# A hybrid encoder step on one core: the convolved tile gets a second buffer, the first tile's products are reordered, and the next tokens' norm is issued earlier

## The chip, the cores and the metric

One core of a Trainium2 chip runs the whole kernel. The metric is device time in microseconds (us), the median of several executions. The engines are TensorE (PE, the matmuls, with its weight loads PEld), VectorE (DVE), ScalarE (ACT), GpSimd (POOL) and SyncE (SP), which issues the DMA transfers. Each engine runs its own queue of instructions in order and waits on semaphores for the others.

## The reference

One layer of a streaming encoder is applied to 2048 prompt tokens and to 32 further tokens of a running stream. The width is 1024. Phase one, which the change is about, is the mixer's input side:

```python
proj = rmsnorm(x, g_mix_pre) @ w_in            # q, k, v: 512 each; z: 512; xbc: 768; dt: 8
xbc_c, conv_new = causal_dwconv(xbc, conv_prev, w, b)   # width 4, along the tokens
xbc_c = silu(xbc_c)                            # 512 of x, 128 of B, 128 of C
dt = softplus(dt_raw + dt_bias)
y, h_fin = ssd_scan(x, dt, -exp(a_log), B, C, h0)       # a state carried from chunk to chunk
y = rmsnorm((y + d_skip * x) * silu(z), g_ssm_out)
```

Then come stick-breaking attention of 8 heads over q, k and v, the output projection, and a GeLU-gated MLP with a convolution of width 3. All arithmetic is float32.

## The kernel before, in words

**Products.** A float32 matrix product is made of three in a faster 32-bit format (`F32R`): each operand is divided into a high part and a low remainder, and high by high, high by low and low by high are summed in PSUM. For the tokens these parts are `xhi[k]` and `xlo[k]`, for k = 0 to 7 (8 x 128 = 1024 rows), in one buffer each (`parts`). For the weights `divide` makes them: ACT writes the high part (L145), POOL the low one (L146). `dense` (L152) issues 24 products of one output tile: for each k, the three in a row.

**Blocks of tokens.** `phase_in` runs over four blocks (`SBS`): three of 512 tokens and a last one of 544. For each block s it does, in the order of the source:

1. `split`: ACT writes xhi from the normalised tokens `x` (L319), DVE the low parts xlo (L320). Block 0 has a helper of its own, `first` (L334, L335).
2. Six output tiles of xbc, in the order c = 4, 5, 0, 1, 2, 3. Each is evicted by ACT into `raw` (L377), convolved by DVE into `xc[:, c]` (L384 and three times L388), and multiplied by its sigmoid (ACT L392, DVE L393). `xc` comes from the pool `kn.xcp`, which has one buffer.
3. v and dt (L412): four or five groups of 128 tokens, two halves of 24 products each, evicted by ACT (L419, L421). In block 0 `load_wv` brings their weights just before.
4. The scan's scalars (L443 to L471), with small products into PSUM tiles `st`, and then the scan itself by groups of 128 tokens (L478 to L562). It reads and overwrites `xc`. The row `acD` goes out to memory and comes back spread over all partitions (`acB`, `eA`).
5. `prep(s + 1)`, not in the last block: four DMA loads of the next tokens into `x` (L299), their squares on ACT (L303, L306) summed by POOL (L307), the root through two PSUM tiles `st` (`rstd_steps`: PE L203, DVE L216, POOL L226, PE L238, ACT L248), and eight DVE products that normalise `x` in place (L310).
6. Four tiles of k and four of q: evicted by ACT or DVE (L352, L350), divided by ACT and POOL (L584, L585), and stored.
7. `gate`: four tiles of z, whose sigmoid multiplies `xc` (ACT L627, DVE L628, L630); and `gate_norm`: squares (L641 to L645), a root (L177 to L183), DVE products on `xc` (L650), and its two parts, made by ACT (L654) and POOL (`klo`, L656) and stored. In the last block these two steps are left to the attention stage.

**Order.** All of it is traced in the order of the source, and then a scheduler puts each engine's instructions in a fixed order by a simulated timeline; the source order is the priority. A tile of a pool is waited for until the last reader of the buffer's previous tile is through. The sizes that matter: the product tiles `o` have two PSUM buffers (shared by steps 2, 3, 6 and 7), `st` has two, and `x`, `raw` and `xc` have one buffer each.

Later stages (attention of all heads, with the rest of the layer as filler work between its steps) keep `xc` until the last block's gate is done, and are not touched by the change.

Of the kernel before, what the change touches and what calls it, by code (L numbers as in the profile page):

```python
# [8 lines left out]
F32 = mybir.dt.float32  # L9
# [22 lines left out]
P = 128  # L32
# [37 lines left out]
class Kernel:  # L70
# [81 lines left out]
    def parts(self):  # L152
        return tuple([self.xp.tile([P, 544], F32R, name=f"{e}{k}") for k in range(KC)] for e in ("xhi", "xlo"))

    def dense(self, ps, w, x, c0, c1, k0=0, first=True, last=True, pin=False, loose=False):
        nc = self.nc
        xhi, xlo = x
        for k, (whi, wlo) in enumerate(w):
            hi, lo = xhi[k0 + k][:, c0:c1], xlo[k0 + k][:, c0:c1]
            for i, (l, r) in enumerate(((whi, hi), (whi, lo), (wlo, hi))):  # L160
                mm = nc.tensor.matmul(  # L161
                    ps[:, : c1 - c0], l, r,
                    start=first and i == 0 and k == 0,
                    stop=last and i == 2 and k == len(w) - 1,
                    **({"skip_group_check": True} if loose else {}),
                )
                if pin and i == 0 and k == 0:
                    self.pin(mm)
        if pin:
            self.mark(mm)  # L170

# [81 lines left out]
def phase_in(kn, ctx):  # L253
    nc, tc, a, o = kn.nc, kn.tc, kn.a, kn.o
# [39 lines left out]
    def prep(s):  # L294

        t0, nt = SBS[s]
        x = ep.tile([P, KC, 544], F32, name="x")
        for k in range(0, KC, 2):
            nc.sync.dma_start(x[:, k : k + 2, :nt], a["xT"][:, k : k + 2, t0 : t0 + nt])  # L299
        sq = tmp.tile([P, 544], F32, name="sq", bufs=1)  # L300
        for k in range(KC):
            if k == 0:
                nc.scalar.activation(sq[:, :nt], x[:, k, :nt], AF.Square)  # L303
            else:
                t = tmp.tile([P, 550], F32, name="t")
                nc.scalar.activation(t[:, :nt], x[:, k, :nt], AF.Square)  # L306
                nc.gpsimd.tensor_tensor(sq[:, :nt], sq[:, :nt], t[:, :nt], op=ALU.add)  # L307
        r = kn.rstd_narrow(rp, psm, "st", [sq], nt, D)
        for k in range(KC):
            nc.vector.scalar_tensor_tensor(  # L310
                x[:, k, :nt], x[:, k, :nt], kn.col(C_GMIX + k), r[:, :nt], op0=ALU.mult, op1=ALU.mult
            )
        return x

    def split(s, x):
        nt = SBS[s][1]
# [38 lines left out]
    for s, (t0, nt) in enumerate(SBS):  # L355
        last = s == NSB - 1
        if s == 0:
            xs, r0 = first()
            rcol = kn.rcol
        else:  # L360
            xs = split(s, nxt)
        xhi, xlo = xs
        raw = ep.tile([P, 6, 550], F32, name="raw")
        xc = kn.xcp.tile([P, 6, 547], F32, name="xc")
        W = 547 if last else 512
        nc.vector.tensor_copy(raw[:, :, 0:3], hist[:])
        if last:
# [3 lines left out]
        for c in (4, 5, 0, 1, 2, 3):  # L371
            w = wfirst if s == 0 and c == 4 else kn.weight(wp, a["wbx"][c])
            for c0, c1 in tiles_of(nt):
                ps = psd.tile([P, 512], F32, name="o")
                kn.dense(ps, w, xs, c0, c1)
                e = min(c1, 512)
                nc.scalar.copy(raw[:, c, 3 + c0 : 3 + e], ps[:, : e - c0])  # L377
                if c1 > 512:
                    nc.scalar.copy(raw[:, c, 518:550], ps[:, e - c0 : c1 - c0])
            if s == 0:  # L380
                nc.vector.tensor_tensor(raw[:, c, 3 : 3 + nt], raw[:, c, 3 : 3 + nt], r0[:, :nt], op=ALU.mult)
            y = xc[:, c, :W]
            wc = C_SW + c * 4
            nc.vector.tensor_scalar(  # L384
                y, raw[:, c, 0:W], kn.col(wc), kn.col(C_SB + c), op0=ALU.mult, op1=ALU.add
            )
            for i in range(1, 4):
                nc.vector.scalar_tensor_tensor(  # L388
                    y, raw[:, c, i : i + W], kn.col(wc + i), y, op0=ALU.mult, op1=ALU.add
                )  # L390
            t = tmp.tile([P, 550], F32, name="t")
            nc.scalar.activation(t[:, :W], y, AF.Sigmoid)  # L392
            nc.vector.tensor_tensor(y, y, t[:, :W], op=ALU.mult)  # L393
# [3 lines left out]
        else:  # L397
            nc.vector.tensor_copy(hist[:], raw[:, :, 512:515])

        if s == 0:  # L400
            load_wv()
        nb = 5 if last else 4
# [3 lines left out]
        for b in range(nb):  # L406
            q = min(P, nt - b * P)
            vp = [psd.tile([P, 512], F32, name="o") for _ in range(2)]
            for h in range(2):
                for k in range(KC):  # L410
                    for i, (l, rr) in enumerate(((xhi, wv[0]), (xlo, wv[0]), (xhi, wv[1]))):
                        nc.tensor.matmul(  # L412
                            vp[h][:q, :260], l[k][:, b * P : b * P + q], rr[:, k, h * 260 : h * 260 + 260],
                            start=i == 0 and k == 0, stop=i == 2 and k == KC - 1,
# [40 lines left out]
        ps = psm.tile([P, 512], F32, name="st")  # L455
# [10 lines left out]
        ps = psm.tile([P, 512], F32, name="st")  # L466
# [6 lines left out]
        for b in range(nb):  # L473
# [22 lines left out]
            for g in range(2):  # L496
                rows = slice(g * 64, g * 64 + 64)
                nc.tensor.matmul(cy[:q, g, :q], xc[rows, 4, sl], xc[rows, 5, sl], start=True, stop=True)
                for i in range(2):
# [3 lines left out]
                        start=True, stop=True,  # L503
# [15 lines left out]
            ps = psm.tile([P, 512], F32, name="st")  # L519
# [11 lines left out]
            ps = psm.tile([P, 512], F32, name="st")  # L531
# [16 lines left out]
            ps = psm.tile([P, 512], F32, name="st")  # L548
# [19 lines left out]
            nc.sync.dma_start(o["ssm"][0], hT[state["h"]][:])  # L568
            nc.sync.dma_start(o["ssm"][1], hS[:])

        if not last:
            nxt = prep(s + 1)
        for name, dst in (("wk", kn.kS), ("wq", kn.qS)):
            for c in range(4):
                w = kn.weight(wp, a[name][c])
                hi = so.tile([P, 544], F32, name="khi")[:].bitcast(F32R)
                lo = so.tile([P, 544], F32, name="klo")[:].bitcast(F32R)
                kf = so.tile([P, 544], F32, name="kf")
                for c0, c1 in tiles_of(nt):
                    ps = psd.tile([P, 512], F32, name="o")  # L580
# [1039 lines left out]
```

## Time and profile before

| | us |
|---|---|
| median of 3 runs | 2937.35 |
| lowest and highest | 2936.06, 2943.05 |
| the profiled execution | 2941.02 |
| its span, first to last instruction | 2939.2 |
| of it TensorE busy | 2814.1 (96%) |
| VectorE, ScalarE, GpSimd busy | 1690.8, 1263.4, 1275.4 |

The profile lists instructions by source line, engine, operation and tile (`o<-xhi,w` writes o from xhi and w). A row of waits says which engine and line stood idle for which other engine and line: in total, how many times, and the longest. A row of the order of time has a start, a duration, the instruction and how many of its kind follow each other, and in brackets the idle time before it with what ended it. A row by stretches gives busy time of each engine and the mean clock that TensorE was granted (1.00 is full). Phase one ends about 640 us into the span.

### The profile page before, as it was taken

Reading aid. Unit: us, or ns where it says so; the run is one execution under the profiler, and the core shown is the slowest. Engines: PE = TensorE matmul, PEld = TensorE weight load, DVE = VectorE, ACT = ScalarE, POOL = GpSimd, SP = SyncE. Lnnn points to the kernel's source line nnn. Section 1 sums busy time; section 2 is a strip of 40 time slices with the busy share of each in tenths; the row PEclk is TensorE's granted clock in tenths of the full one; section 3 lists DMA queues with packets and bytes.
Section 4 is the critical chain, followed back from the end, with each engine's and each line's share of the span. In section 5 each row is a group of like instructions: output and inputs, shape, how many; then the busy total and the mean of one; then the engine's idle time right before and its main releaser. Section 6 shows DMA issues by size and latency. Waiting matters only on the chain.

```text
span 2939.2 us, 46252 instructions
## 1 busy us (share of the span) xinstructions
PE 2814.1 (96%) x16771; PEld 2427.5 (83%) x16771; DVE 1690.8 (58%) x2628; ACT 1263.4 (43%) x2622; POOL 1275.4 (43%) x1131
## 2 busy tenths in 40 slices
PE   7999999989889999999999999999999999999997
PEld 6777777977788888897788888977888889999997
DVE  7667586566773555447555556675666653623333
ACT  4344444337665555446333444654444443321111
POOL 4565555435766666656322323453223233511113
PEclk9999999989999999999999999999999999999999
DMA  5646464648787778777655556656555445765556
GB/s 179 183 137 193 132 176 124 174 115 271 247 282 263 253 263 276 266 256 250 215 180 172 174 180 219 225 182 205 176 172 170 160 159 202 241 181 179 170 178 200
DMA packets 333093, 586.47 MB, mean 200 GB/s; under 512 B 73306, under 2 KB 192738, under 8 KB 332866
## 3 DMA queue, kind: packets, MB, share of 16 engines
q1 hardware_dynamic: 332866, 583.52, 62.1%
q8 instruction: 134, 2.20, 0.3%
q14 instruction: 93, 0.76, 0.1%
HBM read 445.70 MB, written 137.69 MB: 198 GB/s over the span
## 4 chain that ended last, share of the span: by engine, by line
PE 72%; DVE 13%; DMA 7%; ACT 3%; issue 2%; POOL 1%; SPq 1%; DVEq 0%; ACTq 0%; POOLq 0%
PE o L161 35%; PE u L161 12%; PE t L161 10%; PE z L863 4%; PE pa L904 4%; PE pt L882 3%; DVE xc L388 2%; DMA acB<-acD 2%; PE o L412 1%; DVE acB L488 1%; DVE prow L714 1%; DMA xr<-hS 1%; DVE xc L384 1%; DVE xlo L320 1%; DVE x L310 1%
## 5 line engine op out<-in xcount | busy, mean ns | idle before, releaser
L161 PE MATMUL o<-xhi,w 128*128 128x512 f32 (+2 forms) x3968 | 1047.9, 346 | 24.1 <-ACT xhi L334 8.0
L161 PEld LDWEIGHTS o<-xhi,w 128*128 128x128 f32 x3968 | 697.3, 191 | 119.0 <-ACT xhi L334 8.0
L161 PE MATMUL o<-xlo,w 128*128 128x512 f32 (+2 forms) x1984 | 683.8, 345 | 6.3 <-DVE xlo L320 4.2
L146 POOL TENSOR_TENSOR w<-wraw,w 128x512 fp32r<-128x512 f32 (+3 forms) x244 | 384.3, 1577 | 261.4 <-ACT w L145 232.2
L719 POOL TENSOR_TENSOR beta<-beta,prow 128x512 f32<-128x512 f32 (+3 forms) x256 | 252.5, 987 | 442.7 <-DVE prow L714 366.8
L161 PEld LDWEIGHTS o<-xlo,w 128*128 128x128 f32 x1984 | 380.0, 192 | 50.4 <-DVE xlo L320 6.1
L161 PE MATMUL u<-xhi,w 128*128 128x512 f32 x1056 | 350.3, 398 | 0.0
L161 PE MATMUL o<-ah,w 128*128 128x512 f32 x992 | 344.4, 403 | 4.3 <-DVE f L1348 3.8
L1300 POOL TENSOR_TENSOR y<-y,gb 128x512 f32<-128x512 f32 (+1 forms) x88 | 116.0, 1318 | 503.2 <-ACT gb L1299 503.1
L714 DVE TENSOR_TENSOR_SCAN prow<-gam,prow,z 128x513 f32<-128x513 f32 x192 | 245.2, 1278 | 74.1 <-ACT beta L712 69.7
L887 DVE TENSOR_TENSOR wt<-pt,wt 128x512 fp32r<-128x512 f32 (+2 forms) x320 | 191.0, 602 | 159.6 <-ACT wt L886 157.8
L886 ACT CAST wt<-pt 128x512 fp32r<-128x512 f32 (+2 forms) x320 | 166.9, 527 | 218.2 <-PE pt L882 216.3
L145 ACT CAST w<-wraw 128x512 fp32r<-128x512 f32 (+3 forms) x244 | 172.1, 705 | 170.6 <-PE o L161 98.6
L161 PEld LDWEIGHTS u<-xhi,w 128*128 128x128 f32 x1056 | 199.1, 189 | 46.8
L161 PEld LDWEIGHTS o<-ah,w 128*128 128x128 f32 x992 | 187.2, 189 | 47.0 <-DVE f L1348 6.0
L711 ACT ACTIVATE gam<-z 128x512 f32<-128x512 f32 (+2 forms) x320 | 172.3, 538 | 96.0 <-PE z L863 53.9
L161 PE MATMUL u<-xlo,w 128*128 128x512 f32 x528 | 209.5, 397 | 0.0
L161 PE MATMUL o<-al,w 128*128 128x512 f32 x496 | 196.7, 397 | 0.0
L161 PE MATMUL t<-xhi,w 128*128 128x272 f32 x960 | 189.6, 293 | 2.6 <-DMA w<-wS_up 1.7
L882 PE MATMUL pt<-ident,beta 128*128 128x128 f32 x1088 | 180.3, 277 | 4.2 <-DVE wt L887 2.7
L1292 DVE SCALAR_TENSOR_TENSOR y<-gb,cv,y 128x512 f32<-128x512 f32 (+1 forms) x176 | 142.4, 809 | 72.6 <-ACT y L1290 69.9
L904 PE MATMUL pa<-wt,v 128*64 128x256 f32 (+3 forms) x1152 | 172.3, 280 | 8.6 <-DVE wt L887 6.6
(275 smaller groups left out, 4956.4 us busy)
## 6 DMA issues: line engine op xcount, KB each, us to landing
w<-wS_up SPq DMA_DIRECT2D x264, 512.0 KB, 3.6
w<-wS_dn SPq DMA_DIRECT2D x144, 384.0 KB, 3.5
wS_up<-w SPq DMA_DIRECT2D x88, 512.0 KB, 3.4
w<-wS_out SPq DMA_DIRECT2D x78, 512.0 KB, 5.7
wraw<-wup SPq DMA_DIRECT2D x88, 256.0 KB, 4.0
k<-kS SPq DMA_DIRECT2D x80, 256.0 KB, 4.1
v<-vS SPq DMA_DIRECT2D x80, 256.0 KB, 3.8
wS_dn<-w SPq DMA_DIRECT2D x48, 384.0 KB, 3.1
```

The costliest lines, as they stand in the source:

```text
L145: nc.scalar.copy(hi, raw[:, :m, :])
L146: nc.gpsimd.tensor_tensor(lo, raw[:, :m, :], hi.bitcast(F32), op=ALU.subtract)
L161: mm = nc.tensor.matmul(ps[:, : c1 - c0], l, r, start=first and i == 0 and k == 0, stop=last and i == 2 and k == len(w) - 1, **({"skip_gro ...
L711: nc.scalar.activation(g[:, c0:512], z, AF.Sigmoid, scale=-0.125)
L714: nc.vector.tensor_tensor_scan(back(pr), back(g), z[:, 0:1].to_broadcast([P, n + 1]), self.kn.ones[:, 0:1] if prev is None else prev, op0= ...
L719: eng.tensor_tensor(b[:, :n], b[:, :n], pr[:, c0 + 1 : 513], op=ALU.mult)
L863: mm = nc.tensor.matmul(z[:, :n], q[:, P * b : P * b + P], k[:, :n], start=e == 0, stop=e == 1 and kc < s)
L882: mm = nc.tensor.transpose(t[:, P * j : P * j + P], w[:, P * j : P * j + P], kn.ident[:])
L886: nc.scalar.copy(hi, t)
L887: nc.vector.tensor_tensor(lo, t, hi.bitcast(F32), op=ALU.subtract)
L904: nc.tensor.matmul(av[:m, 2 * P * p + c0 : 2 * P * p + 2 * P], v[:, j, :m], wt[:, rest, j, c0:], start=kc == s and p + j + rest == 0, stop ...
L1292: nc.vector.scalar_tensor_tensor(y[:, :W], gb[:, i : i + W], kn.col(wc + i), y[:, :W], op0=ALU.mult, op1=ALU.add)
```

## The change

It has three parts. The convolved tile `xc` gets two buffers. For the tile c = 4, which is the first of each block, `dense` issues the sixteen products that need only `xhi` first and the eight with `xlo` after them. And `prep` becomes a generator: its loads, squares and root are issued ahead of `load_wv`, v and the scan; each of its eight normalising products is then issued ahead of one of the eight tiles of k and q. The number of instructions stays the same.

```diff
-    def dense(self, ps, w, x, c0, c1, k0=0, first=True, last=True, pin=False, loose=False):
+    def dense(self, ps, w, x, c0, c1, k0=0, first=True, last=True, pin=False, loose=False, rests=False):
         nc = self.nc
         xhi, xlo = x
+        terms, late = [], []
         for k, (whi, wlo) in enumerate(w):
             hi, lo = xhi[k0 + k][:, c0:c1], xlo[k0 + k][:, c0:c1]
-            for i, (l, r) in enumerate(((whi, hi), (whi, lo), (wlo, hi))):
-                mm = nc.tensor.matmul(
...
+            terms += [(whi, hi), (wlo, hi)] if rests else [(whi, hi), (whi, lo), (wlo, hi)]
+            late += [(whi, lo)] if rests else []
+        for i, (l, r) in enumerate(terms + late):
+            mm = nc.tensor.matmul(
+                ps[:, : c1 - c0], l, r,
+                start=first and i == 0,
+                stop=last and i == 3 * len(w) - 1,
...
@@ prep
         r = kn.rstd_narrow(rp, psm, "st", [sq], nt, D)
+        yield x
         for k in range(KC):
-            nc.vector.scalar_tensor_tensor(
+            yield nc.vector.scalar_tensor_tensor(
                 x[:, k, :nt], x[:, k, :nt], kn.col(C_GMIX + k), r[:, :nt], op0=ALU.mult, op1=ALU.mult
             )
-        return x
@@ phase_in
-        xc = kn.xcp.tile([P, 6, 547], F32, name="xc")
+        xc = kn.xcp.tile([P, 6, 547], F32, name="xc", bufs=2)
...
-                kn.dense(ps, w, xs, c0, c1)
+                kn.dense(ps, w, xs, c0, c1, rests=c == 4)
...
+        ahead = iter(())
+        if not last:
+            ahead = prep(s + 1)
+            nxt = next(ahead)
         if s == 0:
             load_wv()
...
-        if not last:
-            nxt = prep(s + 1)
         for name, dst in (("wk", kn.kS), ("wq", kn.qS)):
             for c in range(4):
+                next(ahead, None)
                 w = kn.weight(wp, a[name][c])
```

More of the change, by code (lines that the diff above doesn't have):

```diff
@@ L153, in parts @@
         return tuple([self.xp.tile([P, 544], F32R, name=f"{e}{k}") for k in range(KC)] for e in ("xhi", "xlo"))
-    def dense(self, ps, w, x, c0, c1, k0=0, first=True, last=True, pin=False, loose=False):
+    def dense(self, ps, w, x, c0, c1, k0=0, first=True, last=True, pin=False, loose=False, rests=False):
         nc = self.nc
         xhi, xlo = x
+        terms, late = [], []
         for k, (whi, wlo) in enumerate(w):
             hi, lo = xhi[k0 + k][:, c0:c1], xlo[k0 + k][:, c0:c1]
-            for i, (l, r) in enumerate(((whi, hi), (whi, lo), (wlo, hi))):
[L161 to L168, printed above, removed]
+            terms += [(whi, hi), (wlo, hi)] if rests else [(whi, hi), (whi, lo), (wlo, hi)]
[5 more added lines that the diff above has]
+                stop=last and i == 3 * len(w) - 1,
+                **({"skip_group_check": True} if loose else {}),
+            )
+            if pin and i == 0:
+                self.pin(mm)
         if pin:
```

## The prediction

> **What bounds the kernel now.** I read the page's totals first, then busy time by stage, then TensorE's waits inside phase one, then the order of time on each engine around the longest of them.
>
> ```profile
> span 2939.2 us, 46252 instructions
> PE 2814.1 (96%) x16771; PEld 2427.5 (83%) x16771; DVE 1690.8 (58%) x2628; ACT 1263.4 (43%) x2622; POOL 1275.4 (43%) x1131
> ```
>
> TensorE (PE) carries the kernel. The stage table has one row for each block of tokens of phase one (cut where its parts xhi begin to be written) and one for all that follows; the columns are the stretch, its length, busy time and instructions of PE, its weight loads, DVE, ACT and POOL, PE's granted clock, DMA's share and GB/s:
>
> ```profile
> 0.00:170.00 170.00, 149.27 (x793) 120.50 (x794) 117.73 (x196) 71.02 (x104) 81.72 (x56) 0.98 0.55 169
> 170.00:327.00 157.00, 147.19 (x794) 117.86 (x793) 102.32 (x172) 68.41 (x107) 91.15 (x53) 0.98 0.55 161
> 327.00:488.00 161.00, 149.88 (x812) 119.92 (x811) 113.87 (x173) 72.78 (x113) 91.35 (x54) 0.99 0.53 160
> 488.00:640.00 152.00, 139.55 (x1065) 130.56 (x1064) 93.81 (x173) 55.11 (x103) 65.29 (x44) 0.93 0.51 143
> 640.00:2939.00 2299.00, 2228.24 (x13314) 1938.68 (x13312) 1263.10 (x1918) 996.06 (x2198) 945.87 (x925) 0.99 0.65 211
> ```
>
> Behind 640 us PE is 97% busy and the change touches nothing, so what phase one gains or loses should reach the end whole. In phase one PE is idle 54 of 640 us (the four rows: 640 less 149.3, 147.2, 149.9 and 139.6). No other engine is full over a block (DVE at most 71%), so these are waits of an order, not of a bound. They are, on PE up to 650 us (total, times, longest):
>
> ```profile
> PE o L412 <- ACT v L421: 8.9, 3, 3.4
> PE y L538 <- DVE acB L510: 5.1, 5, 2.7
> PE o L161 <- DVE t L628: 5.1, 2, 2.6
> PE st L532 <- DVE hT L562: 4.6, 2, 3.5
> PE o L161 <- DVE xlo L320: 4.2, 3, 1.8
> PE o L161 <- DVE xlo L335: 1.2, 1, 1.2
> PE o L412 <- ACT raw L379: 0.9, 1, 0.9
> PE o L161 <- ACT sq L641: 0.9, 1, 0.9
> ```
>
> The reader should sort them by part of the change: v's products held by ACT (8.9 and 0.9), the first tile held by the low parts (4.2 and 1.2), the gate's products held by DVE (5.1 and 0.9). The scan's own waits (L538, L532) are touched by none.
>
> **The change, part by part.**
>
> *Two buffers for xc.* In block 1 the last raw tile, then the order of time on DVE, ACT and PE, and below it busy time before and after DVE is let go:
>
> ```profile
> 210.66 0.59 ACT L377 COPY raw<-o 128x512 f32<-128x512 f32 x1 [4.11 <-PE o L161]
> 207.49 4.44 DVE L384 TENSOR_SCALAR xc<-raw,cv 128x512 f32<-128x512 f32 x5 [5.64 <-POOL klo L656]
> 223.34 1.29 ACT L392 ACTIVATE t<-xc 128x512 f32<-128x512 f32 x2 [5.28 <-DVE xc L388]
> 224.95 0.39 PE L412 MATMUL o<-wvhi,xhi 128*128 128x260 f32 x1 [2.88 <-ACT v L421]
> 187.00:207.00 20.00, 20.00 (x85) 15.40 (x84) 7.99 (x5) 11.00 (x15) 13.98 (x9) 1.00 0.65 214
> 207.00:232.00 25.00, 22.06 (x168) 20.97 (x167) 24.51 (x32) 7.50 (x14) 15.05 (x7) 1.00 0.51 145
> ```
>
> The convolution of block 1 can't write xc until gate_norm of block 0 has read it for the last time (klo, L656). It starts at 207.5 although DVE was busy 8 of the 20 us before, then fills DVE (24.5 of 25). ACT, in order, sits 5.28 us at a sigmoid whose convolution isn't done; v's eviction stands behind it; both o buffers are full; PE waits 2.88. With a second buffer the six chains (some 25 us together) can go along with the products: the last raw tile is evicted at 211, the first five tiles of 24 products earlier (85 in 20 us make 5.6 us a tile), near 183. The end comes at 211 plus one chain of 4 us and a sigmoid: about 216 instead of 232. Gain: up to 8.9 + 0.9 = 9.8 of idle. What is late next is that last chain, which still overlaps v's first two evictions. I take off 1 us for each of three blocks (between nothing and the 3.3 each has now; nearer nothing, since one chain is left of several): **-6.8**, ends -9.8 and 0.
>
> *First tile by parts.* The same 24 products; the eight with xlo go last, so that the other sixteen need xhi alone.
>
> ```profile
> 328.11 9.69 DVE L320 TENSOR_TENSOR xlo<-x,xhi 128x512 fp32r<-128x512 f32 x7
> 337.85 0.50 PE L161 MATMUL o<-xlo,w 128*128 128x512 f32 x1 [1.81 <-DVE xlo L320]
> 19.36 0.74 PE L161 MATMUL o<-xhi,w 128*128 128x512 f32 x2 [0.66 <-POOL w L146]
> ```
>
> Between 338 and 340 PE waits twice for low parts of which DVE writes seven in 9.69 us. Each low part is now needed later by up to the sixteen products that use none, 3.8 us at that pace, and the waits here sum to 2.5: **-4.2**, ends -4.2 and 0 (PE could stand at xhi instead; between blocks it has no such wait now). In block 0 I take nothing of the 1.2: the second tile begins at 19.36, held by POOL's low weights, whenever the first ends.
>
> *Root ahead of v, products dealt over k and q.* Nothing is added or removed: four x loads, eight squares on ACT, seven sums on POOL, small products, a power and eight DVE products for each of three blocks.
>
> ```profile
> 244.78 1.29 POOL L307 TENSOR_TENSOR sq<-sq,t 128x512 f32<-128x512 f32 x1
> 302.71 0.15 DVE L216 TENSOR_SCALAR rn_v<-st 128x4 f32<-128x4 f32 x1
> 310.30 7.54 DVE L310 SCALAR_TENSOR_TENSOR x<-x,cv,rstd 128x512 f32<-128x512 f32 x8 [0.45 <-ACT rstd L248]
> 317.77 1.27 DVE L628 TENSOR_TENSOR t<-o,t 128x512 f32<-128x512 f32 x2
> 318.59 0.48 PE L161 MATMUL o<-xhi,w 128*128 128x512 f32 x1 [2.64 <-DVE t L628]
> L299 SPq DMA_DIRECT2D x<-xT x12: 378/462/937, 21.5 to 341.0; - x12
> ```
>
> The sum is ready at 246; its root comes at 302.7, behind the scan, whose st tiles of PSUM stand first in the source; then eight products in one piece hold DVE while the gate's o buffers wait. Dealt earlier, the 5.1 and 0.9 go: **-6.0**, ends -6.0 and 0. The loads are moved in the source past wv's (block 0), v's, the scan's and SP's other requests, but they are issued already at 21.5, as soon as x is free; I take nothing for the queue. If they did delay wv, the price would be one landing, 6 us in the median. The squares compete with v's evictions on ACT and the sums with v's low parts on POOL, as they do now.
>
> Two costs. The eight products (7.54 us in one block, 22.6 in three) land in the scan, where DVE waits 39.8 us in all for acB from DMA:
>
> ```profile
> L488 DVE TENSOR_SCALAR acB<-acB,acum 128x128 f32<-128x128 f32 (+1 forms) x136 | 51.6, 445 | 39.8 <-DMA acB<-acD 39.8
> L310 DVE SCALAR_TENSOR_TENSOR x<-x,cv,rstd x24: 739/748/2926, 159.2 to 482.5; 128x512 f32<-128x512 f32 x16, 128x544 f32<-128x544 f32 x8
> ```
>
> That hides most; were the cover gone, it would cost all 22.6. Single products took up to 2.9 us (minimum, median, maximum in ns above), so not every one fits its hole: **+2**, ends 0 and +22.6. And the root's small products now stand in PE's order close to the sums they need, and in the ring of two st tiles ahead of the scan's; a wait there holds all behind it on PE, and the scan's first products through st. Before, it had 50 us of slack and no wait. Bounds: nothing, and 3.4 in each of three blocks, the longest wait of PE for ACT above. I take 1 each, nearer nothing, since the readiness that ordered the loads will order it too: **+3**, ends 0 and +10.
>
> *Clock.* PE's busy time and granted clock beside some of these waits:
>
> ```profile
> 225.00:230.00 5.00, 5.00 (x42) 1.00 0.45 114
> 315.00:320.00 5.00, 2.36 (x10) 0.95 0.37 107
> 320.00:325.00 5.00, 5.00 (x17) 0.71 0.34 105
> 340.00:345.00 5.00, 5.00 (x17) 0.66 0.87 297
> 545.00:550.00 5.00, 5.00 (x31) 0.68 0.76 195
> ```
>
> A wait of 2.64 us is followed by 5 x 0.05 + 5 x 0.29 = 1.7 us lost to the clock; the xlo waits by 5 x 0.34 = 1.7; block 3's v wait by 1.6; that of 2.88 at 224 by none. All three are behind waits that should go: **-5.0**, ends -5.0 and 0. The Trainium skill ("TensorE: Matmul & The Clock Gate", Part 1) says that the clock is halved after an idle window of about 3.4 us, and that waits below 3 us are safe; by it none of these waits would have cost clock, and the sum would be 5 us poorer, -12. The trace disagrees: 2.64 us did.
>
> **Sum**: -6.8 - 4.2 - 6.0 + 2 + 3 - 5.0 = -17.0. The profiled execution took 2941.0 us (span 2939.2 and 1.8 around it), 3.7 above the median of 2937.35. So 2924.0 for that execution, and 2920.3 against the median.
>
> **The rivals.**
>
> *The wait moves.* The convolution goes from after POOL's klo to beside it (POOL is busy 14.0 of 20 us from 187 to 207). DVE runs slower, ACT meets the sigmoids between the evictions of raw, and PE waits for o there. For it: L384 has a median of 545 ns and a maximum of 2645 in blocks 1 to 3, so DVE does get held; against: DVE has 12 free us of 20 there. Then the first term is 0 and its 1.6 of clock stays: 2920.3 + 6.8 + 1.6 = 2928.7. The Trainium skill ("SBUF — State Buffer", Who interferes with whom) bears on this: DVE instructions with two SBUF inputs and GpSimd's reads exclude each other for a whole instruction; the slow L310 and L384 fit that, though L384 has one tensor input.
>
> *The scan sets the end.* If the dealt products lengthen the chain acB, y, hT by their whole 22.6 instead of 2, the end is 2920.3 + 20.6 = 2940.9: no change. For it: L538 and L532 already make PE wait; against: the scan waits on DMA rather than on DVE.
>
> *Slower: the root stands in PE's queue before its sum.* If its products are placed ahead of v's, PE stops from there to the last square: block 0 from 53.7 to 81.9, 28 us; blocks 1 and 2 from 211 to the sum's present end, 246, less the 16 by which the convolution is done sooner, so 19 to 20 each. That gives 68 us in place of 3: 2985. It decides, against 20.0 of gain without the root, from 28.8 us in all (8.8 is 0.3%), 9.6 a block. Against it: the loads, placed in the source behind the scan, ran before it, so queues follow readiness and not the source. These times of PE and POOL come from here:
>
> ```profile
> 53.66 0.39 PE L412 MATMUL o<-wvhi,xhi 128*128 128x260 f32 x1 [1.72 <-ACT raw L377]
> 80.69 1.25 POOL L307 TENSOR_TENSOR sq<-sq,t 128x512 f32<-128x512 f32 x1
> ```
>
> That the change doesn't do what it says can be only in the third part, if the scheduler places the dealt products as before; then its terms are 0 and 1.7 of clock stays: about 2923, inside the forecast.
>
> **How the numbers follow.** Chances: forecast 0.62, the wait moves 0.17, the scan 0.12, the root 0.09. Less than 0.3% (8.8 us, edges 2928.5 and 2946.2) can't be told from no change. Faster: 0.60 of the forecast's 0.62 and half of the second, 0.09, make 0.69; slower: 0.09 and 0.02 of the scan, 0.11; same 0.20. The best ends give -25.0, 2912; 6 us more if block 3's scan (waits of 3.5 and 2.7) also loosens: low 2906. High 2938: it takes in the second rival and half of the third, and leaves out the root, the rest of the scan and 0.04 below. The likeliest case's own range is 2908 to 2929.
>
> **What the changed profile would show.** Right: no DVE wait of xc L384 for klo; PE's waits on ACT in v's products below 3 us in blocks 1 to 3 together; none of the first tile on xlo L320; L310 in single instructions during k and q, L216 before the scan; clock 1.00 where 0.66 to 0.71 stood. Wrong: PE waits at L203 or L238, waits for raw L377 between the first six tiles, longer waits at L538, L532 and L500, or a stage behind 640 us of other length (the larger xc shifts what lies beside it, which no row here prices).

## The result, and the profile after

The changed kernel is slower: 2955.16 us (median of 4, 2951.07 to 2958.63) against 2936.7 (median of 4) for the kernel before on the same chip, a ratio of 1.0055 (95% interval 1.0035 to 1.0076). The forecast was 2920.3. The profiled execution took 2954.74 us with this span, in the totals of the page:

```profile
span 2952.9 us, 46271 instructions
PE 2818.1 (95%) x16771; PEld 2430.5 (82%) x16771; DVE 1713.1 (58%) x2628; ACT 1260.9 (43%) x2622; POOL 1273.0 (43%) x1131
```

The same 2628 DVE instructions take 22 us longer. By stage, at the same cuts as before:

```profile
0.00:170.00 170.00, 150.66 (x802) 120.27 (x803) 117.72 (x196) 73.04 (x108) 82.97 (x56) 0.98 0.55 169
170.00:327.00 157.00, 140.83 (x752) 112.97 (x751) 107.29 (x167) 63.36 (x99) 83.36 (x52) 0.96 0.53 155
327.00:488.00 161.00, 148.46 (x793) 119.30 (x792) 112.62 (x167) 68.26 (x106) 90.61 (x53) 0.97 0.52 158
488.00:640.00 152.00, 136.87 (x1000) 126.36 (x999) 101.10 (x162) 57.91 (x105) 67.13 (x43) 0.96 0.51 143
```

PE does fewer products in blocks 1 to 3 (752, 793 and 1000 for 794, 812 and 1065). Its clock is lower in blocks 1 and 2 (0.96 and 0.97 for 0.98 and 0.99) and higher in the stretch of block 3 (0.96 for 0.93). Tile by tile, the last z tile of block 1 ends 7.8 us later than before, that of block 2 12.3, the last q tile of block 3 17.4 (663.6 for 646.2). From there the i-th matmul counted from the end stays 16 to 19 us late until 2100 us and is 14.4 late at 2900: the whole loss is made in phase one. Up to the last q tile both kernels run the same 3509 instructions on PE (the kernel before, then the changed kernel):

```profile
0.00:646.20 646.20, 592.10 (x3509) 495.04 (x3510) 427.73 (x710) 268.74 (x427) 330.87 (x207) 0.97 0.54 158
0.00:663.60 663.60, 600.42 (x3509) 500.69 (x3510) 445.79 (x709) 267.10 (x427) 330.23 (x207) 0.96 0.52 154
```

PE is idle for 63.2 us where it was idle for 54.1, and busy for 600.4 where it was busy for 592.1. So 9.1 us of the 17.4 are waiting, and the other 8.3 are the same products taking longer, which the granted clock fits (0.96 for 0.97). PE's waits up to 650 us (total, times, longest):

```profile
PE o L419 <- ACT raw L380: 12.6, 5, 4.4
PE y L545 <- DVE acB L517: 8.5, 6, 3.6
...
PE o L164 <- POOL w L146: 7.2, 8, 1.8
PE o L164 <- DVE xlo L323: 5.5, 4, 2.4
PE st L539 <- DVE acT L476: 4.8, 3, 2.6
...
PE o L164 <- ACT raw L382: 3.8, 1, 3.8
PE o L419 <- ACT v L426: 3.2, 2, 2.3
PE o L164 <- ACT w L145: 3.1, 1, 3.1
...
PE o L164 <- DVE t L631: 0.2, 1, 0.2
```

The waits that the change aimed at were not saved but renamed: v waits for ACT's evictions of raw (12.6) where it waited for those of v (8.9); with the smaller rows v's products wait 15.8 us in all where they waited 14.7. A convolved tile of block 3 waits 3.8 for raw, the weights' low parts cost 7.2 where they cost 1.9, acB 8.5 where 5.1, and acT's 4.8 and a weight's high part (3.1, in block 0) are new. Only the gate's products (t, 5.1 to 0.2) came out as forecast. In block 1 the order of time shows how (two stretches):

```profile
181.29 0.55 DVE L387 TENSOR_SCALAR xc<-raw,cv 128x512 f32<-128x512 f32 x1 [1.17 <-ACT raw L380]
181.88 6.16 DVE L391 SCALAR_TENSOR_TENSOR xc<-raw,cv,xc 128x512 f32<-128x512 f32 x3
182.95 2.83 POOL L146 TENSOR_TENSOR w<-wraw,w 128x1024 fp32r<-128x1024 f32 x1
188.13 0.63 ACT L395 ACTIVATE t<-xc 128x512 f32<-128x512 f32 x1 [5.39 <-DVE xc L391]
188.66 0.57 ACT L380 COPY raw<-o 128x512 f32<-128x512 f32 x1
189.13 1.05 ACT L145 CAST w<-wraw 128x1024 fp32r<-128x1024 f32 x1
...
221.34 0.63 ACT L395 ACTIVATE t<-xc 128x512 f32<-128x512 f32 x1 [5.49 <-DVE xc L391]
221.87 0.57 ACT L380 COPY raw<-o 128x512 f32<-128x512 f32 x1
222.50 0.59 PE L419 MATMUL o<-wvhi,xhi 128*128 128x260 f32 x1 [4.40 <-ACT raw L380]
```

The convolution does start at 181 instead of 207, as the second buffer should allow. But its three multiply-adds now take 6.16 us beside POOL's subtraction, ACT stands 5.39 us at the sigmoid, and the eviction of raw and the next weight's high part stand behind the sigmoid on ACT. At 221 the same thing holds v, and the clock falls in the two stretches around and behind that wait:

```profile
220.00:225.00 5.00, 2.50 (x11) 2.50 (x12) 3.90 (x7) 2.33 (x4) 1.54 (x1) 0.61 0.21 82
225.00:230.00 5.00, 5.00 (x33) 5.00 (x32) 3.42 (x5) 2.05 (x4) 2.33 (x2) 0.71 0.34 105
```

DVE's groups of multiply-adds and ACT's waits for them, 165 to 650 us, before (L388, L392) and after (L391, L395):

```profile
L388 DVE SCALAR_TENSOR_TENSOR xc<-raw,cv,xc 128x512 f32<-128x512 f32 (+1 forms) x54 | 45.8, 903 | 0.0
ACT t L392 <- DVE xc L388: 21.5, 5, 6.2
ACT t L392 <- DVE xc L393: 10.2, 7, 3.7
```

```profile
L391 DVE SCALAR_TENSOR_TENSOR xc<-raw,cv,xc 128x512 f32<-128x512 f32 (+1 forms) x54 | 72.4, 1351 | 1.3
L323 DVE TENSOR_TENSOR xlo<-x,xhi 128x512 fp32r<-128x512 f32 (+1 forms) x24 | 31.0, 1345 | 1.0 <-ACT xhi L322 1.0
ACT t L395 <- DVE xc L391: 64.1, 18, 5.9
```

903 ns became 1351 (the column behind the busy time), 26.6 us more in three blocks, more than DVE's gain of 22 in the totals. ACT waits at all eighteen sigmoids, 64 us for 32. The changed kernel's trace also shows what sets the slow ones apart: 24 of the 54 multiply-adds overlap no POOL instruction and take 740 to 790 ns each; the other 30 take 1823 ns on average, up to 2878. Of the twenty that take over 900 ns, 15 run beside subtractions of weights, 8 beside gate_norm's klo and 3 beside the sums of squares (some beside two of these); with one buffer the convolution came behind klo.

### The profile page after: what moved, and what is told of

It is laid out like the page before. It is cut to its first block, busy times and chain, and to the rows that moved or that the text cites. A ratio compares the mean times of both kernels' runs of the same rounds, so it can differ in the third digit from the quotient of the medians.

```text
span 2952.9 us, 46271 instructions
## 1 busy us (share of the span) xinstructions
PE 2818.1 (95%) x16771; PEld 2430.5 (82%) x16771; DVE 1713.1 (58%) x2628; ACT 1260.9 (43%) x2622; POOL 1273.0 (43%) x1131
## 4 chain that ended last, share of the span: by engine, by line
PE 75%; DVE 13%; DMA 6%; issue 2%; ACT 2%; SPq 1%; POOL 1%; DVEq 0%; ACTq 0%; POOLq 0%
PE o L164 36%; PE u L164 12%; PE t L164 10%; PE pa L910 4%; PE z L869 4%; PE pt L888 4%; PE o L419 3%; DVE xc L391 2%; DMA acB<-acD 1%; DMA xr<-hS 1%; DVE prow L720 1%; DVE x L314 1%; DVE xlo L1058 1%; DVE acB L495 1%; DVE xlo L323 1%
## 5 line engine op out<-in xcount | busy, mean ns | idle before, releaser
L717 ACT ACTIVATE gam<-z 128x512 f32<-128x512 f32 (+2 forms) x320 | 172.7, 540 | 94.7 <-PE z L869 54.1
```

The source lines that it names most:

```text
L717: nc.scalar.activation(g[:, c0:512], z, AF.Sigmoid, scale=-0.125)
```

## The experiments

Each is compared with runs of the kernel before on its own chip (medians 2935 to 2941). "Phase one" is the end of the last q tile against the kernel before, "late" what the matmuls lose from 1300 to 1700 us, both from the one profiled execution of each kernel. A few us of either can be chance: 29 executions of the kernel before on one chip spread over 2929 to 2949 us, and the profiled execution lies 10.5 us under the median in e9 and 9.8 over it in e13.

| kernel | median us | ratio (95%) | phase one | late |
|---|---|---|---|---|
| after | 2955.2 | 1.0055 (1.0035, 1.0076) | +17.4 | 0 |
| e1_buf | 2956.2 | 1.0062 (1.0044, 1.0081) | -1.2 | +12 |
| e2_parts | 2937.0 | 1.0009 (0.9993, 1.0026) | -2.5 | 0 |
| e3_root | 2941.4 | 1.0011 (0.9998, 1.0025) | +2.1 | 0 |
| e4_root_parts | 2940.2 | 1.0006 (0.9992, 1.0019) | -0.2 | 0 |
| e5_buf_root | 2960.1 | 1.0082 (1.0061, 1.0103) | +17.9 | 0 |
| e6_buf_parts | 2955.6 | 1.0067 (1.0044, 1.0089) | -5.5 | +14 |
| e7_root_later | 2970.0 | 1.0116 (1.0092, 1.0140) | +16.1 | +12 |
| e16_root_undealt | 2961.7 | 1.0095 (1.0070, 1.0121) | +19.0 | +1 |
| e17_dealt_only | 2955.4 | 1.0080 (1.0051, 1.0110) | +0.6 | +12 |
| e9_lag2 | 2956.7 | 1.0055 (1.0038, 1.0072) | +10.6 | +1 |
| e8_no_low | 2902.2 | 0.9880 (0.9855, 0.9905) | -31.6 | -1 |
| e11_no_low_before | 2917.3 | 0.9909 (0.9876, 0.9941) | -23.1 | +1 |
| e12_kept | 2948.0 | 1.0025 (1.0007, 1.0042) | +6.2 | -1 |
| e13_kept_before | 2935.5 | 0.9991 (0.9972, 1.0010) | -1.7 | -1 |
| e18_kept3 | 2945.1 | 1.0029 (1.0010, 1.0048) | -12.8 | +12 |
| e19_lag_same_order | 2955.6 | 1.0056 (1.0039, 1.0072) | +17.4 | -1 |
| e20_kept3_buf | 2915.9 | 0.9920 (0.9905, 0.9935) | -16.5 | 0 |
| e21_kept3_lag | 2913.3 | 0.9910 (0.9893, 0.9927) | -19.9 | +2 |

**One part at a time.** Each adds one part of the diff to the kernel before.

```diff
 e1_buf
+        xc = kn.xcp.tile([P, 6, 547], F32, name="xc", bufs=2)
 e2_parts
+                kn.dense(ps, w, xs, c0, c1, rests=c == 4)
 e3_root
+            ahead = prep(s + 1); nxt = next(ahead)     # before load_wv; next(ahead) in k and q
```

> Only the second buffer of xc, all else as before. Buffer theory (the convolution now runs beside POOL's weight parts, takes longer, and ACT stands at its sigmoids with evictions and weight casts behind them): this alone is slower, 2947 to 2960 us, and ACT's waits at the convolution's sigmoid for DVE are near 60 us as in the changed kernel, against some 30 before. Root theory (the early root holds the scan through the ring of two st tiles, and that is the loss): the buffer alone is a gain, 2925 to 2933 us.

> Only the order of the first tile's products (those with xlo last), all else as before. Both theories: a small gain from the 4.2 us of waits for xlo and at most 1.7 us of clock behind them, 2931 to 2936 us. If it is slower than 2943 us, a third theory is needed: the order of the products costs by itself.

> Only the root ahead of v and its products dealt over k and q, all else as before. Buffer theory: gain or nothing, 2926 to 2938 us, although the scan's first small products (L456 of the kernel before) come after the root's. Root theory: 2948 to 2956 us, with the scan starting some 10 us later after v in block 0 and PE waiting for it.

Parts and root alone change nothing that can be measured. The buffer alone ends v of block 1 6.6 us later, yet has made it up by that block's last z; its total is lost elsewhere (below), so it fell into the range of its first theory for another reason than that theory's. The root alone has one clear price, the wait for acB (5.1 before), on PE up to 650 us in e3_root:

```profile
PE y L545 <- DVE acB L517: 12.1, 7, 3.0
```

**Two at a time.** The changed kernel less one part.

```diff
 e4_root_parts
-        xc = kn.xcp.tile([P, 6, 547], F32, name="xc", bufs=2)
 e5_buf_root
-                kn.dense(ps, w, xs, c0, c1, rests=c == 4)
 e6_buf_parts
-            ahead = prep(s + 1); nxt = next(ahead)     # prep back behind the scan, undealt
```

> The changed kernel with one buffer for xc again (order of products and early root kept). Buffer theory: the loss goes and the two small gains remain, 2922 to 2936 us. Root theory: still slow, 2946 to 2956 us.

> Second buffer and early root together, products of the first tile in the old order. In the profiles phase one's last product of q ends at 646 us before, at 664 in the changed kernel, at 645 with the buffer alone and at 646 with root and parts alone. Pair theory (buffer and root lose only together: the buffer delays v by 7 to 11 us, the scan that could give this back starts later still because of the root): phase one ends at 658 to 666 us. Buffer-alone theory as first put (DVE beside POOL costs phase one by itself) is already contradicted by 645; if this run ends at 640 to 650 us, the parts are what is missing. Total only loosely: 2945 to 2960 us.

> Second buffer and the first tile by parts, root where it was. Pair theory: phase one ends at 640 to 648 us, as with the buffer alone; the total depends on the order that the attention stage then gets (2930 to 2955 us). If it ends above 655 us, the parts and not the root make the loss with the buffer.

The total of e2 lies 1 us above its range, those of e3 and e4 lie 3 to 4 us above the ranges of the buffer theory and well below those of the root theory. Neither theory alone holds; the pair makes the loss of phase one. The buffer costs nothing alone (-1.2), the root little (+2.1), the two together 17.9, which is all of the changed kernel's 17.4. Up to the last q tile PE is idle 53.8 us with the buffer, 56.5 with the root and 62.7 with both (54.1 before), and busy 591.2, 591.9 and 601.4 with the same products (592.1 before): the pair costs waiting and clock in like parts. One place where the two meet is the scan. Block 1 of the changed kernel:

```profile
254.11 1.05 PE L241 MATMUL st<-ident,rn_v 128*128 128x128 f32 x8
255.82 4.74 DVE L314 SCALAR_TENSOR_TENSOR x<-x,cv,rstd 128x512 f32<-128x512 f32 x4
258.94 0.27 PE L474 MATMUL st<-ident,acum 128*32 128x128 f32 x1
264.47 2.74 DVE L314 SCALAR_TENSOR_TENSOR x<-x,cv,rstd 128x512 f32<-128x512 f32 x4
267.55 0.27 DVE L476 COPY acT<-st 32x128 f32<-32x128 f32 x1
267.85 0.34 SPq L478 DMA_DIRECT2D acD<-acT  x1
275.77 1.66 DVE L495 TENSOR_SCALAR acB<-acB,acum 128x128 f32<-128x128 f32 x8 [6.98 <-DMA acB<-acD]
285.77 1.86 PE L545 MATMUL y<-acB,xdt 128*64 128x128 f32 x16 [3.65 <-DVE acB L517]
```

and of e1_buf, where the root comes behind the scan:

```profile
256.13 0.27 PE L467 MATMUL st<-ident,acum 128*32 128x128 f32 x1
257.51 0.28 DVE L469 COPY acT<-st 32x128 f32<-32x128 f32 x1
257.82 0.34 SPq L471 DMA_DIRECT2D acD<-acT  x1
264.59 4.16 DVE L488 TENSOR_SCALAR acB<-acB,acum 128x128 f32<-128x128 f32 x8 [6.08 <-DMA acB<-acD]
273.48 1.09 PE L538 MATMUL y<-acB,xdt 128*64 128x128 f32 x16
```

The root being ready, its eight products stand on DVE ahead of acT: PE has transposed the row at 259, DVE copies it at 267.6, and the way out to memory and back starts 10 us later than in e1_buf. The scan's first y comes at 285.8 for 273.5. From the end of v to the last y blocks 0 to 2 take 81, 73 and 77 us, for 68, 64 and 63 before. What that does to PE, in us from the first product of xbc to the end of v, and from there to the end of z (in block 3: of q):

| | block 1 | block 2 | block 3 |
|---|---|---|---|
| before | 63.5, 93.9 | 67.1, 91.0 | 73.7, 82.8 |
| e1_buf | 72.3, 85.4 | 67.4, 89.1 | 76.0, 82.7 |
| e3_root | 64.4, 94.4 | 66.5, 92.8 | 75.0, 78.8 |
| after | 73.1, 94.0 | 70.7, 91.9 | 79.7, 81.9 |
| e5_buf_root | 72.7, 95.7 | 71.3, 92.4 | 79.7, 80.8 |
| e17_dealt_only | 72.6, 84.5 | 68.5, 91.7 | 74.5, 81.7 |

In block 1 the buffer costs some 9 us up to v and, with the root late, gives 8.5 back behind it. With the root early nothing comes back; in the changed kernel the scan's head is late there, and PE stands at acT and acB. The other 9 or so are lost up to v in blocks 2 and 3 (3.6 and 6.0). That DVE comes to these blocks late from the scan and gate of the block before, so that xlo and the convolution are late, fits the waits for xlo (5.5) and raw; no run takes it apart.

**Which half of the third part?** The root behind the scan's scalars (e7); early, but the products undealt (e16); dealt, but loads and root behind the scan as before (e17).

```diff
 e7_root_later
+        yield x                                         # in prep, now ahead of the root
         r = kn.rstd_narrow(rp, psm, "st", [sq], nt, D)
-        yield x
+        yield
...
         nc.sync.dma_start(acd[:n8, :], acT[:n8, :])
+        next(ahead, None)
 e16_root_undealt
-                next(ahead, None)
+        for _ in ahead: pass                            # behind k and q
 e17_dealt_only
-            ahead = prep(s + 1); nxt = next(ahead)     # before load_wv
+            ahead = prep(s + 1); nxt = next(ahead)     # behind the scan
```

> The changed kernel, but the root's small products issued behind the scan's scalars (after the row acD is sent off) instead of ahead of v; loads and squares stay ahead. If the ring of the two st tiles holds the scan: its first small product comes 6 to 9 us after v's last one in every block (19.5, 9.8 and 10.8 in blocks 0 to 2 of the changed kernel), and phase one ends at 648 to 658 us. If the loss is only DVE beside POOL and the dealt products: the scan starts sooner and phase one ends above 660 us all the same.

> The changed kernel, root early, but the eight products of each block in one piece behind k and q, ahead of the gate. Dealing theory (the products on DVE lengthen the scan, and with v later by the second buffer there is no slack left for it): the time from v's last product to the scan's last y falls from 73 us in block 1 to 60 to 66, and phase one ends at 643 to 652 us (664 in the changed kernel). Early-root theory (squares, sums and root between v and the scan's scalars hold it): it stays at 70 us or more and phase one ends above 658 us.

> The changed kernel with loads, squares and root issued behind the scan as before, and only the products dealt over k and q. Dealing theory: phase one still ends at 658 us or later, if the scheduler lets the products run in the scan at all. Early-root theory: it ends at 643 to 652 us. If the root comes after the scan as in the kernel before (its last small product near 309 us in block 1), the dealt products can't come earlier, and this run then equals buffer and parts alone (641 us).

It is the early root: without it +0.6 (e17), with it and undealt +19.0 (e16). The dealing in the source does not matter, for the products run when the root is ready (257 to 268 in e16, 316 to 323 in e17). e7 missed: the scalars come early enough there (8 to 9 us behind v), but the root's small products then stand before the groups' transposes through the same two st tiles, and phase one still loses 16.1. PE has no wait for acT there and 2.1 us for acB, less than before (5.1), while its waits for xlo (5.5) and for low weights (7.7) are near those of the changed kernel. So the late copy of acT is not the whole of what the early root costs. How the loss divides between the st tiles and DVE's queue is not settled.

**The convolution beside POOL.** e8 (the change) and e11 (the kernel before) fill the low parts of the six convolved tiles' weights with zeros instead of subtracting, so that part of the product is left out. e9 keeps all work and only places each sigmoid on ACT behind the eviction of the tile after next.

```diff
 e8_no_low, e11_no_low_before
-        nc.gpsimd.tensor_tensor(lo, raw[:, :m, :], hi.bitcast(F32), op=ALU.subtract)
+        nc.gpsimd.memset(lo.bitcast(F32), 0.0)          # the six tiles of wbx only
 e9_lag2
+            due.append(c)
+            if len(due) > 2:
+                silu(due.pop(0), gone)                  # gone: the eviction of raw just issued
```

> The changed kernel, with the low parts of the six convolved tiles' weights filled with zeros by GpSimd instead of subtracted (so these low products add nothing; all instructions of the other engines stay). If GpSimd's reads hold the convolution on DVE: the three multiply-adds fall from a mean of 1351 ns towards 900 or below in blocks 1 to 3, ACT's waits at the sigmoid from 64 us below 45, and phase one ends 5 to 15 us sooner than 664. If DVE is slow for another reason: the mean stays above 1200 ns.

> The kernel before, with the low parts of the six convolved tiles' weights filled with zeros by GpSimd instead of subtracted (their low products add nothing). The changed kernel with the same filling took 2902 us, 53 less than without it. Contention theory (the second buffer is harmful only because it puts the convolution beside GpSimd's subtractions): here, where the convolution waits for gate_norm and meets few of them, the filling gains less, 5 to 25 us: 2912 to 2932 us; the change is then a gain of 8 to 25 us once the subtractions are away. If this comes to 2897 to 2907 us too, the filling gains by itself and the second buffer is worth nothing even without contention.

> The changed kernel with each convolved tile's sigmoid held on ScalarE behind the eviction of the tile after next, so that evictions and weight casts no longer stand behind it. If ACT's order turns DVE's slowness into PE's waits: ACT's waits at the sigmoid fall below 30 us, PE's waits for raw and for low weights in blocks 1 to 3 fall by half, phase one ends 8 to 20 us sooner than 664. If DVE's own time is the bound: ACT waits less, but v's first evictions wait for the last sigmoids as before and phase one ends at 658 us or later.

With these reads of POOL gone the changed kernel's convolution is faster and phase one 49 us shorter (e8, 165 to 650 us):

```profile
L394 DVE SCALAR_TENSOR_TENSOR xc<-raw,cv,xc 128x512 f32<-128x512 f32 (+1 forms) x54 | 55.1, 1027 | 1.2
ACT t L398 <- DVE xc L394: 45.2, 15, 4.8
```

1351 ns fell to 1027 with the same arithmetic on DVE. The direction was expected, the sizes were not (towards 900 or below, and 5 to 15 us). Of the 49 us 31 are PE's idle time and 18 its busy time, so more than the convolution changed: PE waits less for low weights (4.4 for 7.2), and a third of these tiles' products now have a zero operand, whose effect on the clock no run separates. The kernel before gains too, but less. By the ratios of e11 and e8 (0.9909 and 0.9880) the change is worth some 8.5 us once these subtractions are away, as in phase one (31.6 less 23.1); the two intervals overlap, so that this gain is not shown. The order on ACT is not shown to matter: in e9 PE's waits for raw almost go (2.1 for 16.4), but those for low weights are 8.5, the scan waits 11.7 for the convolved tiles, and the 7 us that the profiled execution has less in phase one are all busy time (591.8 for 600.4), not waiting. Its median is that of the changed kernel, 2956.7 for 2955.2, and its sibling e19 lost by the same edit.

**The subtractions made once.** The divided weights of the six tiles are stored in block 0 and loaded again in blocks 1 to 3, in the changed kernel (e12) and the kernel before (e13), then before with three buffers for divided weights (e18).

```diff
 e12_kept, e13_kept_before, e18_kept3
-            w = ... kn.weight(wp, a["wbx"][c])
+            w = ... kn.weight(wp, a["wbx"][c], key=("bx", c))
 e18_kept3
-            kn.wp, kn.unit, kn.wbufs, kn.rbufs = ..., KC, 2, 2
+            kn.wp, kn.unit, kn.wbufs, kn.rbufs = ..., KC, 3, 2
```

> The changed kernel; the divided weights of the six convolved tiles are stored in memory in block 0 and loaded again in blocks 1 to 3 (no cast by ScalarE and no subtraction by GpSimd there; 0.5 MB more for each load and 6 MB of stores). Contention theory: as with the zeros, the multiply-adds near 1030 ns or below, phase one ends 20 to 50 us sooner than 664; total 2900 to 2935 us. If the larger loads come too late, PE waits for them and the gain is gone: 2945 us or more.

> The kernel before with the same stored and loaded weights. Contention theory: a smaller gain than for the changed kernel, 2915 to 2935 us, so that the change as a whole gains 5 us or more on this base. If it is as fast as the changed kernel with stored weights, or faster, the three parts are worth nothing even there.

> The kernel before with the six convolved tiles' divided weights stored and loaded again, and three buffers instead of two for divided weights. PE waited 10.5 us for these loads with two buffers; with three they can be issued one tile of products (5.6 us) sooner. If that is what held the gain back: 2915 to 2930 us. If the stores of block 0 (phase one 7 us later there) and the longer loads cost as much as they save: 2930 to 2940 us.

With two buffers the loads come late (PE waits 7.4 and 10.5 us for them) and eat what POOL saves. On this base the change still loses (e12 1.0025, e13 0.9991), although its multiply-adds are down to 1127 ns; this is the case for which e13's expectation says that the three parts are worth nothing even there. PE's waits for acB (7.9) and acT (4.8) remain in e12, so the contention with these subtractions is not the whole loss. With three buffers and the kernel before, phase one is 12.8 us shorter, and the total is 8 us longer, outside both ranges; the next part says where it goes. The third buffer holds all of phase one's weights, and a kernel with three buffers and no stored weights was not run.

**Where five totals go.** e1, e6, e7, e17 and e18 lose 12 to 14 us between 1300 and 1700 us, in the attention stage, which none of them edits. Busy time there, the kernel before and e1_buf:

```profile
1400.00:1500.00 100.00, 96.29 (x461) 78.91 (x460) 52.33 (x80) 37.01 (x78) 31.98 (x30) 0.98 0.65 204
```

```profile
1400.00:1500.00 100.00, 88.81 (x425) 72.59 (x424) 49.69 (x75) 34.24 (x74) 33.09 (x29) 0.95 0.62 192
```

In these five 1308 of 2080 PE products between 1300 and 1700 us are in another order than before, the same other order in all five; in the kernels without the loss the order there is that of before (in e13 a third one, which costs nothing). The last three kernels have two buffers and the order of before: e19 is e6 with e9's edit; e20 is e6 with e18's; e21 has both.

```diff
 e20_kept3_buf: the kernel before, and
+        xc = kn.xcp.tile([P, 6, 547], F32, name="xc", bufs=2)
+                kn.dense(ps, w, xs, c0, c1, rests=c == 4)
+            w = ... kn.weight(wp, a["wbx"][c], key=("bx", c))
+            kn.wp, kn.unit, kn.wbufs, kn.rbufs = ..., KC, 3, 2
```

> Two buffers and the first tile by parts (as e6_buf_parts, 2955.6), and each sigmoid of the convolution queued on ACT behind the eviction of the tile after next. The order of PE's products between 1300 and 1700 us of this kernel is that of the kernel before, product by product, where e6_buf_parts differs in 1308 of 2080. Theory A (the 14 us that e1, e6, e7, e17 and e18 lose between 1300 and 1700 us are the price of that order): no loss there, phase one 5 to 10 us sooner than before, total 2927 to 2932. Rival B (two buffers for xc cost those 14 us by themselves, by where things lie or by the squares and gate falling otherwise): the loss comes with the buffer whatever the order, total 2941 to 2950.

> Two buffers, first tile by parts, the convolved tiles' divided weights stored in block 0 and reloaded in blocks 1 to 3 into one of three buffers (two before): POOL makes no low part beside the convolution in these blocks. The order of PE's products between 1300 and 1700 us is that of the kernel before. Theory A: phase one of e18_kept3 (12.8 us sooner without the second buffer) plus what the buffer gives when POOL is quiet (15 us between e11 and e8, of it 6 to 8 without the root): 16 to 20 sooner, kept to the end, total 2917 to 2925, faster than both kernels. Rival B (order is not the cause): 14 of it lost again by 1700 us, total 2930 to 2940.

> As e20_kept3_buf with the sigmoids queued behind later evictions as in e19. The order of PE's products between 1300 and 1700 us is that of the kernel before. Theory A: 14 to 22 sooner than before at the end of phase one, total 2915 to 2925; if ACT's order is what is left of the loss, below e20, if the free POOL already lets the sigmoids pass, equal to it within 3 us. Rival B: 2930 to 2940.

None of the three loses there. Nor do the changed kernel, e5 and e16, which have the second buffer, while e18 has one buffer and loses. So the loss goes with that order and not with the buffer; what in the order costs the time no run takes apart (in e1_buf PE waits 18.6 us there for 8.3, at a clock of 0.98 for 1.00). e19's total missed all the same: its phase one is 23 us longer than e6's, 6.0 us of it idle time of PE and 16.9 busy time with the same 3509 instructions, at a clock of 0.95 for 0.98. The sigmoids' places leave a new wait at the scan, in its list of PE's waits up to 650 us:

```profile
PE y L516 <- DVE xc L384: 8.6, 2, 5.3
```

e20 and e21 compute everything and are faster than both kernels, and than the kernel before by 0.8% and 0.9%; they end 1 and 2 us below their ranges. What the stored weights, the third buffer and the second xc buffer with the parts are each worth in the total is not separated, since e18, the step between, has the other order. In e20, 165 to 650 us, and PE's waits up to 650:

```profile
L391 DVE SCALAR_TENSOR_TENSOR xc<-raw,cv,xc 128x512 f32<-128x512 f32 (+1 forms) x54 | 59.0, 1101 | 1.2
L323 DVE TENSOR_TENSOR xlo<-x,xhi 128x512 fp32r<-128x512 f32 (+1 forms) x24 | 17.1, 753 | 0.8 <-ACT xhi L322 0.7
PE o L415 <- ACT raw L380: 8.1, 3, 3.8
PE o L164 <- POOL w L146: 5.1, 4, 2.4
```

The multiply-adds are at 1101 ns, and the waits for raw and w both below those of the changed kernel (12.6 and 7.2). Some 9 us more than at the end of phase one are gained by 750 us, in the last block's gate; that was not followed up.

## Why the prediction was wrong, step by step

In the prediction's own terms waiting was to change by -6.8 - 4.2 - 6.0 + 2 + 3 = -12.0 us and the clock to give -5.0. Up to the end of phase one the changed kernel shows +9.1 of waiting and +8.3 of busy time for the same products. Both had the wrong sign.

*Two buffers for xc: -6.8 forecast, the first step that failed.* Alone the buffer brought -1.2 in phase one (e1). The start came as said and no multiply-add waits for klo any longer, but "six chains (some 25 us together)" were costed at the durations of the old place. Beside POOL's subtractions the multiply-adds took half as long again; block 1's convolution ended at 228 rather than "about 216 instead of 232", and v's first two tiles took 12.7 us of PE's time, from the start of the first product to that of the last, where they took 5.6. v ended 7.6 us later. The rival that the wait moves named this mechanism, POOL, ACT and the place, and was priced as a gain forgone rather than a loss. e8 shows its cause: with those reads of POOL away 1351 ns become 1027. The Trainium skill ("SBUF — State Buffer", Who interferes with whom), cited there as a fit, is borne out by these two numbers and by the 740 to 790 ns clear of POOL, for its rule on two SBUF inputs, though its list of operations doesn't name this one.

*Root: +2 and +3 forecast, the second step that failed.* "The scan waits on DMA rather than on DVE" was true of its middle, not of its head: the products fell in front of the one small copy (acT, 0.27 us) from which the DMA's round trip starts. Scans became 9 to 14 us longer in three blocks, where I had 2 in all. Alone that cost PE little (e3, +2.1), as v to z of block 1 took 94 us in either order. What it takes away in block 1 is the stretch in which the buffer's loss is made up; that the late copy does it is argued from the trace, and e7, where PE doesn't wait for acT, loses nearly as much. The two costs do not add: -1 and 2 make 18, and my sum had them as separate terms, each against the kernel before. The rival that the scan sets the end had this mechanism; its 20.6 is near what e5 lost in phase one, but it was set against gains that weren't there, so that nearness is luck. The sum also took nothing for the moved requests: a weight of block 0 comes 2.8 to 3.2 us late in the changed kernel, e3, e4, e5 and e16, and in none of before, e1, e2 and e6.

*Root ahead, gate's waits: -6.0.* They went (0.2 left), and acB's and acT's waits took their place; e3 and e4 show no gain in time.

*First tile by parts: -4.2.* In e2 the waits for xlo fell from 4.2 to 2.8, those for POOL's w rose from 1.9 to 4.2; phase one gained 2.5, the total nothing measurable. In the changed kernel xlo itself is late (waits of 5.5), DVE being behind.

*Clock: -5.0 forecast, the third step that failed.* At the three places 1.00, 1.00 and 0.97 stand where 0.71, 0.66 and 0.68 stood, but the clock falls behind the new waits: to 0.61 and 0.71 around the 4.40 us at 222.5, to 0.66 from 285 to 290 behind 3.65, to 0.69 from 540 to 545 behind 3.78. The term counted only waits that go and none that come. The length of a wait alone doesn't tell what follows either: in the kernel before 2.88 us at 225 and 3.43 us at 386 lost nothing (1.00), and the prediction named only the first of them. The changed kernel at the three places:

```profile
320.00:325.00 5.00, 5.00 (x23) 3.99 (x22) 1.39 (x2) 1.88 (x3) 1.21 (x2) 1.00 0.51 157
340.00:345.00 5.00, 4.47 (x20) 3.26 (x18) 5.00 (x4) 2.58 (x4) 4.43 (x3) 1.00 0.19 73
545.00:550.00 5.00, 5.00 (x38) 4.73 (x37) 4.11 (x6) 1.94 (x4) 1.48 (x2) 0.97 0.30 105
```

*The rival that ended slower*, the root standing in PE's queue before its sum, did not happen: PE shows no such wait. "A stage behind 640 us of other length" was named as a way to be wrong; it did not decide the changed kernel, but 12 to 14 us in five of its relatives.

## What to carry to other kernels

Before a step is moved beside another engine's work, cost it at the duration it has beside that work, not at its old place, and look at what stands behind its consumer in an in-order queue. Costs that are each hidden need not be hidden together: of a move that costs nothing alone, ask which stretch hides it, and what the other moves take from the same stretch. Beside an engine's waits compare its busy time for the same number of products: here nearly half of the loss was in it. And when a small edit changes a total, first see whether the stage that was edited changed: here an untouched stage moved by 14 us.

## What the runs showed of the hardware that I had not expected

DVE instructions with two inputs from SBUF are slowed by POOL's subtractions far more than the shares of busy time suggest: POOL was busy about half the time, and the multiply-adds went from 903 to 1351 ns on average, the token subtractions (xlo) from 753 in e20 to 1345 in the changed kernel. Clear of POOL a multiply-add never took more than 790 ns, neither before nor after, and beside it up to 2920. The first step of the convolution, with a single tensor input, shows it too: 541 to 564 ns clear of POOL in the changed kernel, up to 2643 beside it.
